# One DMA for each key page and each tile of key rows, in a decoder step on one core

## The chip, the cores and the metric

The kernel runs on one core of a Trainium2 chip. The time is the device time of one execution in microseconds. A core has TensorE (PE in the profile; PEld is its loading of weights), VectorE (DVE), ScalarE (ACT), GpSimd (POOL) and SyncE (SP), each with a list of instructions that it works off in order, and 16 DMA engines that they share. The rows SPq are SP's own queue: it issues DMAs and waits for what they depend on.

## The reference: what is computed

One step of a two-layer decoder trunk in fp32, for a new sequence of 512 tokens and for 8 running sequences of 4 new tokens each with 256 cached tokens. Layer 0 mixes with a convolution module, layer 1 with stick-breaking attention, and each is followed by a gated feed-forward network. What the change touches is in layer 1:

```python
k_past = [jnp.take(cache_k[a], page_table, axis=0).reshape(db, past_len, N_HEADS, HEAD_DIM) ...]
qkv = (h @ attn_w_qkv[a]).reshape(b, t, 3, N_HEADS, HEAD_DIM)
z = jnp.einsum('bqhd,bkhd->bhqk', q, k) * (HEAD_DIM ** -0.5) + bias
log_fail = jnp.where(valid, jax.nn.log_sigmoid(-z), 0.0)
after = lax.cumsum(log_fail, axis=3, reverse=True) - log_fail
weights = jnp.where(valid, jnp.exp(jax.nn.log_sigmoid(z) + after), 0.0)
out = jnp.einsum('bhqk,bkhd->bqhd', weights, v)
```

The cached keys lie in pages of 128 tokens x 16 heads x 64 floats (512 KB); each running sequence has two pages, named by a table, so there are 16. The key rows of the new tokens, 512 x 1024 floats for the long sequence, are an output too (k_p).

## The kernel before

Activations are kept transposed, features on the 128 partitions and 544 tokens (512 + 32) along the free axis, in 8 chunks of 128 features. Weights come in loads of up to 1 MB (`raw`, two buffers, L361), which ACT and DVE split into a high and a low part (L398, L401) for matmuls in three products.

From the attention on (L2111 to L2565) the order of the work is made by a planner, `Plan`. Each step is put down with an engine, a cost in us, and what it reads and writes; `run` (L192) then lists the steps greedily by their estimated times and emits them in that order, so each engine's list is fixed when the program is built. For a step of SP the cost says when its result is there, while SP itself is taken to be free again after 0.7 us (L242). A step with an engine name of its own, such as the flight of a page (L2261, 6.0 us), only delays its users.

Key pages. `key_page` (L2041) fetches a page into one of three buffers in xT, which is free at that time because its content was saved to DRAM (L1896). Pages 0 to 2 are asked for ahead of the attention (L1901), pages 3 to 15 in it (`page`, L2251), each when its buffer has been read. The fetch makes four DMAs, one for each column group x of four heads: partitions 32x to 32x+31 take the tokens 32q + p in four blocks q of 256 floats. DVE transposes the page in blocks of 32 x 32 (L2283), so that the head features lie on partitions, and PE multiplies it with the queries (L2301): `page_logits(m)` does four pages, m = 0 to 3, in matmuls of 128 or 256 columns. After the key pages the value pages come through the same three buffers by POOL's indirect DMAs (L2050).

Key rows. `keys(c, h)` projects the keys of chunk c for half h of the tokens (16 tiles in all). ACT copies the result to kT (L2201), DVE transposes the 256 columns into `kr` (two buffers, L2207), and `store` (L2209) writes it to k_p with four DMAs, one for each 32 features. In DRAM a token's 32 features are a run of 128 B.

Other DMAs that matter for the argument. All go through SP's queue in the order of its list: the weight loads of L361, the stores of values (L2228), and in layer 0 the stores of L1181, which write 32 partitions (8 sequences x 4 tokens) to a DRAM tensor in which the sequences lie 30 rows apart:

```python
dst = sc_s[0, :, PAST - NI:PAST, :].rearrange("b t (h j d) -> b t h j d", h=2, j=4)
nc.sync.dma_start(out=dst[:, :, :, j, :], in_=r)
```

Of the kernel before, what the change touches and what calls it, by code (L numbers as in the profile page):

```python
# [17 lines left out]
P = 128  # L18
D = 1024
NC = D // P  # L20
# [85 lines left out]
class Plan:  # L106
# [5 lines left out]
    def __init__(self, eager=EAGER, chain=0.0, shifts=""):  # L112
        self.eager = eager
        self.shifts = shifts

        self.chain = chain
        self.ops = []
        self.writes, self.adds, self.reads = {}, {}, {}
        self.rings = {}
        self.follows = {}  # L120
        self.lift, self.urgent = {}, {}
        self.forms, self.change = {}, 0.0
        self.fill = set()

    def op(self, eng, cost, fn, r=(), w=(), a=(), follows=None, lift=0.0, urgent=0.0, after=(), form=None):

        i = len(self.ops)
        deps = set(after)
        for x in r:
            deps |= self.writes.get(x, set()) | self.adds.get(x, set())  # L130
        for x in a:
            if self.reads.get(x):
                self.writes[x] = self.writes.get(x, set()) | self.reads[x] | self.adds.get(x, set())
                self.reads[x], self.adds[x] = set(), set()
            deps |= self.writes.get(x, set())
        for x in w:
            deps |= self.writes.get(x, set()) | self.reads.get(x, set()) | self.adds.get(x, set())
        for x in r:
            self.reads.setdefault(x, set()).add(i)
        for x in a:  # L140
            self.adds.setdefault(x, set()).add(i)
        for x in w:
            self.writes[x], self.reads[x], self.adds[x] = {i}, set(), set()
        for x in (*r, *w, *a):
            b = x[0] if isinstance(x, tuple) else x
            if isinstance(b, Plan.Buf):
                if not b.users and b.before is not None:
                    b.after |= {b.before.users[0]}
                if not b.users and b.old is not None:
                    b.after |= set(b.old.users)  # L150
                deps |= b.after
                b.users.append(i)
        deps.discard(i)
        self.ops.append((eng, cost, fn, deps))
        if lift:
            self.lift[i] = lift
        if urgent:
            self.urgent[i] = urgent
        if follows is not None:
            self.follows[i] = follows  # L160
        if form is not None:
            self.forms[i] = form
        return i

    class Buf:
# [26 lines left out]
    def run(self):  # L192
        n = len(self.ops)
        users = [[] for _ in range(n)]
        left = [0] * n
        for i, (_, _, _, deps) in enumerate(self.ops):
            left[i] = len(deps)
            for d in deps:
                users[d].append(i)
        rank = [0.0] * n  # L200
        for i in range(n - 1, -1, -1):
            eng, cost, _, _ = self.ops[i]
            rank[i] = cost + self.lift.get(i, 0.0) + max((rank[u] + self.lag(eng, self.ops[u][0]) for u in users[i]), default=0.0)
        for x in self.shifts.split():
            i, d = x.split(":")
            self.urgent[int(i)] = self.urgent.get(int(i), 0.0) + float(d)
        ready = {}
        start = [0.0] * n
        for i in range(n):
            if not left[i]:  # L210
                ready.setdefault(self.ops[i][0], []).append(i)
        free, last, form = {}, {}, None

        def turned(i):
            return self.change if self.change and self.ops[i][0] == "pe" and self.forms.get(i) != form else 0.0

        while any(ready.values()):
            best = None
            for eng, q in ready.items():
                if q:  # L220
                    f = free.get(eng, 0.0)
                    soon = min(max(f, start[i]) for i in q) + NEAR

                    def key(i):
                        t, turn = max(f, start[i]), turned(i)
                        later = t > soon or i in self.fill or (turn and self.fill and form is None and start[i] + PATIENT > soon)
                        return (bool(later), t + CHANGE_BIAS * turn - self.eager * rank[i] - self.urgent.get(i, 0.0) -
                                (STICK if self.follows.get(i, -1) == last.get(eng) else 0.0), i)

                    i = min(q, key=key)  # L230
                    t = max(f, start[i])
                    if best is None or t < best[0]:
                        best = (t, i, eng)
            t, i, eng = best
            ready[eng].remove(i)
            _, cost, fn, _ = self.ops[i]
            fn()
            cost += turned(i)
            if eng == "pe":
                form = self.forms.get(i)  # L240
            last[eng] = i
            free[eng] = t + (cost if eng != "sp" else 0.7)  # L242
            for u in users[i]:
                left[u] -= 1
                start[u] = max(start[u], t + cost + self.lag(eng, self.ops[u][0]))
                if not left[u]:
                    ready.setdefault(self.ops[u][0], []).append(u)
# [3 lines left out]
def tile_trunk(  # L251
# [8 lines left out]
    nc = tc.nc  # L260
    dve, act, pool, pe = nc.vector, nc.scalar, nc.gpsimd, nc.tensor
# [1778 lines left out]

    def key_page(t, j):  # L2041

        pages = cache_k[0, bass.ds(numbers[j], 1)].rearrange("o (q p) (x h) d -> o x p q (h d)", p=32, x=4)
        for x in range(4):
            nc.sync.dma_start(out=t[32 * x:32 * x + 32, :].rearrange("p (q r) -> p q r", q=4), in_=pages[0, x])

    cv = cache_v.rearrange("o n p h d -> (o n p) (h d)")

# [149 lines left out]
    def keys(c, h):  # L2198
        c0, n = (SA, SB)[h]
        pt = project(k0 + TURNS.index(("k", c)), h)  # L2200
        plan.op("act", acost(256), lambda: act.copy(kT[:, c, c0:c0 + 256], pt()[:, :256]),  # L2201
                r=[pt], w=[("k", c, h)] + ([("ktp", i) for i in range(4)] if c >= 4 else []))
        if h:
            plan.op("act", 0.2, lambda: act.copy(kT_s[:, c, :], pt()[:, 256:n]), r=[pt], w=[("kT_s", c)])
            plan.op("pool", 1.2, lambda: place_k(c), r=[("kT_s", c)], w=[("kn", c)])
        kr = sbuf("kr", 2 * P, 2)
        plan.op("dve", 0.15 + 256 * 1.1e-3, lambda: dve.transpose(kr(), kT[:, c, c0:c0 + 256]), r=[("k", c, h)], w=[kr])  # L2207

        def store():  # L2209
            for a in range(4):  # L2210
                rows = slice(32 * a, 32 * a + 32)
                nc.sync.dma_start(out=k_p[0, 0, c0:c0 + 256].rearrange("(b i) h d -> i b (h d)", i=32)[:, :, c * P + 32 * a:c * P + 32 * a + 32],
                                  in_=kr()[rows].rearrange("i (b j) -> i b j", j=32))

        plan.op("sp", 7.0, store, r=[kr])

    def values(c, h):
        n = (SA, SB)[h][1]
# [12 lines left out]
    def new_rows(src, r, dst):  # L2231

        rows = psum("one")

        def turn():
            for x in range(4):
                for j in range(2):
                    pe.matmul(rows()[HALF[j], x * HD:(x + 1) * HD], src[HALF[j], 2 * x:2 * x + 2, :].rearrange("p c t -> p (c t)"),
                              ident[HALF[j], HALF[j]], start=(x == 0), stop=(x == 3), skip_group_check=True)

        def store():
            for u in range(4):
                nc.sync.dma_start(out=dst.rearrange("t (x u d) -> t u x d", x=4, u=4)[:, 2 * (u % 2) + u // 2],
                                  in_=new_s[32 * u:32 * u + 32].rearrange("p (x d) -> p x d", x=4))

        plan.op("pe", 0.5, turn, r=r, w=[rows], form="r64")
        plan.op("act", 0.35, lambda: act.copy(new_s, rows()[:, :2 * P]), r=[rows], w=["new", "Qz"])
        plan.op("sp", 3.0, store, r=["new"])


    def page(i):  # L2251
# [3 lines left out]
            plan.op("held", 0.0, lambda: None, w=[t])  # L2255
            return t
        if i < 2 * NB:
            plan.op("sp", 2.0, lambda: key_page(t(), i), w=[t, ("asked", i)])
        else:
            plan.op("pool", 1.05, lambda: gather(t(), i % (2 * NB), cv), w=[t, ("asked", i)])  # L2260
        plan.op(f"page{i}", 6.0 if i < 2 * NB else 4.0, lambda: None, r=[("asked", i)], w=[(t, 1)])  # L2261
# [8 lines left out]
    def page_logits(m):  # L2270
# [17 lines left out]
        def logits():  # L2288
            for odd in range(2):
# [5 lines left out]
                    parts = [(0, KW, kt)]  # L2295
                for e in range(2):
                    for lo, n, src in parts:
                        keys_of = src.rearrange("p (q k j) -> p k q j", k=NC, j=32)
                        for u in range(4):
                            k = 4 * (u % 2) + 2 * (u // 2) + e  # L2300
                            pe.matmul(z()[32 * u:32 * u + 32, (m % 2) * KW + lo:(m % 2) * KW + lo + n],  # L2301
# [322 lines left out]
```

## Time and profile before

| | |
|---|---|
| time, median of 3 runs | 1256.89 us (1256.1 to 1257.56) |
| the profiled execution's own time | 1256.83 us |
| its span, first to last instruction | 1255.1 us |
| PE, DVE, ACT, POOL busy | 1239.3, 1011.2, 709.8, 173.8 us |
| granted PE clock | 0.998 |
| DMA packets of SP's queue | 133134 (120.29 MB) |
| key page DMAs / key row DMAs | 64 x 128 KB / 64 x 32 KB |

A row of a group or of the timeline gives line, engine and operation, then out<-in by the program's names. In square brackets stands the idle time just before an instruction, and what ended it. DMA share is the mean busy share of the 16 DMA engines; "share of 16 engines" is the time that a queue's packets took, over 16 times the length of the window.

### The profile page before, as it was taken

To read this page: it belongs to the slowest core of one execution; us is meant where nothing else is said; L and a number is where in the kernel's file an instruction comes from. 1 tells how busy PE (TensorE), PEld (TensorE's weight loads), DVE (VectorE), ACT (ScalarE), POOL (GpSimd) and SP (SyncE) were. 2 spreads that over 40 slices of the span, in tenths; PEclk is the share of its full clock that TensorE was granted. 3 is DMA by queue.
4 is the path that set the end of the run, shared out by engine and by line. 5 is a ranking of instruction groups with operands and counts; after the bars stand their busy time and mean duration, and the time that the engine had idled before them with its cause. 6 is when DMAs were issued, how large, how long until landed. Compare 5 with 4: busy or idle time off the path is not lost.

```text
span 1255.1 us, 26652 instructions
## 1 busy us (share of the span) xinstructions
PE 1239.3 (99%) x10742; PEld 1187.2 (95%) x10742; DVE 1011.2 (81%) x1700; ACT 709.8 (57%) x1421; POOL 173.8 (14%) x363
## 2 busy tenths in 40 slices
PE   9999999999999999999999999999999999999997
PEld 8997699999999999999988888999999999999997
DVE  7999887988987886878969897646979987887863
ACT  7793584646655454445545887744636645455453
POOL 5000014111001000000242344000101001000000
PEclk9999999999999999999999999999999999999999
DMA  7455423123233233244379465232123232233121
GB/s 223 129 168 152 129 68 117 35 86 114 80 112 118 68 106 99 92 145 161 97 190 246 128 173 159 71 126 85 49 88 102 93 120 93 80 108 118 60 79 72
DMA packets 139661, 142.40 MB, mean 113 GB/s; under 512 B 24045, under 2 KB 132773, under 8 KB 139266
## 3 DMA queue, kind: packets, MB, share of 16 engines
q1 hardware_dynamic: 133134, 120.29, 32.1%
q0 software_dynamic: 6400, 20.41, 5.2%
q8 instruction: 84, 1.38, 0.5%
q14 instruction: 39, 0.32, 0.1%
q10 hardware_dynamic: 4, 0.01, 0.0%
HBM read 129.34 MB, written 12.18 MB: 113 GB/s over the span
## 4 chain that ended last, share of the span: by engine, by line
PE 81%; DVE 14%; DMA 2%; ACT 2%; issue 1%; SPq 0%; POOL 0%; DVEq 0%; ACTq 0%
PE acc L1635 5%; PE acc L1634 5%; PE acc L1633 5%; PE acc L759 4%; PE acc L760 4%; PE acc L761 4%; PE av L896 3%; DVE wlo L401 3%; PE av L1412 3%; PE av L1413 3%; PE av L1414 3%; PE tr L1413 3%; PE tr L1412 3%; PE tr L1414 3%; PE tr L1633 3%; PE tr L1635 3%
## 5 line engine op out<-in xcount | busy, mean ns | idle before, releaser
L398 ACT CAST whi<-raw 128x1024 fp32r<-128x1024 f32 (+2 forms) x247 | 224.7, 913 | 123.5 <-PE av L1413 24.8
L401 DVE TENSOR_TENSOR wlo<-raw,whi 128x1024 fp32r<-128x1024 f32 (+2 forms) x247 | 258.7, 1050 | 33.0 <-ACT whi L398 31.5
L759 PE MATMUL acc<-XH,whi 128*128 128x288 f32 (+1 forms) x384 | 112.7, 294 | 0.0
L761 PE MATMUL acc<-XH,wlo 128*128 128x288 f32 (+1 forms) x384 | 110.3, 287 | 0.9 <-DVE wlo L401 0.9
L760 PE MATMUL acc<-XL,whi 128*128 128x288 f32 (+1 forms) x384 | 110.3, 287 | 0.0
L1412 PE MATMUL av<-HH,whi 128*128 128x288 f32 (+1 forms) x280 | 83.2, 297 | 0.5 <-DVE xT L1735 0.5
L1413 PE MATMUL av<-HL,whi 128*128 128x288 f32 (+1 forms) x280 | 82.6, 295 | 0.0
L1635 PE MATMUL acc<-TH,wlo 128*128 128x272 f32 x288 | 82.6, 287 | 0.0
L1634 PE MATMUL acc<-TL,whi 128*128 128x272 f32 x288 | 82.6, 287 | 0.0
L1633 PE MATMUL acc<-TH,whi 128*128 128x272 f32 x288 | 82.5, 287 | 0.0
L1414 PE MATMUL av<-HH,wlo 128*128 128x288 f32 (+1 forms) x280 | 82.2, 293 | 0.0
L1682 ACT COPY G<-acc 128x272 f32<-128x272 f32 (+1 forms) x72 | 26.8, 372 | 93.8 <-PE acc L1635 93.8
L2163 PE MATMUL acc<-XH,whi 128*128 128x256 f32 (+1 forms) x264 | 79.7, 302 | 0.0
L1412 PE MATMUL tr<-HH,whi 128*128 128x256 f32 (+1 forms) x280 | 78.5, 280 | 0.0
L1413 PE MATMUL tr<-HL,whi 128*128 128x256 f32 (+1 forms) x280 | 78.4, 280 | 0.0
L1414 PE MATMUL tr<-HH,wlo 128*128 128x256 f32 (+1 forms) x280 | 78.3, 280 | 0.0
L2165 PE MATMUL acc<-XH,wlo 128*128 128x256 f32 (+1 forms) x264 | 75.7, 287 | 0.0
L2164 PE MATMUL acc<-XL,whi 128*128 128x256 f32 (+1 forms) x264 | 75.7, 287 | 0.0
L759 PEld LDWEIGHTS acc<-XH,whi 128*128 128x128 f32 x384 | 72.2, 188 | 1.4 <-issue 0.4
L761 PEld LDWEIGHTS acc<-XH,wlo 128*128 128x128 f32 x384 | 72.1, 188 | 1.1 <-DVE wlo L401 1.1
L760 PEld LDWEIGHTS acc<-XL,whi 128*128 128x128 f32 x384 | 72.2, 188 | 0.3
L1573 DVE SCALAR_TENSOR_TENSOR cv<-G,fprm,cv 128x560 f32<-128x560 f32 x88 | 69.5, 797 | 0.5
(464 smaller groups left out, 4343.0 us busy)
## 6 DMA issues: line engine op xcount, KB each, us to landing
raw<-in_ffn_w_gate_dram SPq DMA_DIRECT2D x22, 1024.0 KB
raw<-in_ffn_w_up_dram SPq DMA_DIRECT2D x22, 1024.0 KB
raw<-in_ffn_w_down_dram SPq DMA_DIRECT2D x24, 768.0 KB
raw<-in_attn_w_qkv_dram SPq DMA_DIRECT2D x12, 1024.0 KB
xT<-in_cache_k_dram SPq DMA_DIRECT2D x64, 128.0 KB
raw<-in_conv_w_in_dram POOLq DMA_DIRECT2D x6, 1024.0 KB, 6.8
rep<-glu SPq DMA_DIRECT2D x36, 142.0 KB
raw<-in_conv_w_out_dram POOLq DMA_DIRECT2D x4, 1024.0 KB, 6.4
```

Of the source, the lines that this page charges most:

```text
L398: act.copy(hi[:, k, :], src[:, k])
L401: dve.tensor_tensor(lo[:, k, :], src[:, k], hi[:, k, :], op=ALU.subtract)
L759: pe.matmul(o, hi[:, k, :], XH[:, k, c0:c0 + n], start=(k == 0), stop=False)
L760: pe.matmul(o, hi[:, k, :], XL[:, k, c0:c0 + n], start=False, stop=False)
L761: pe.matmul(o, lo[:, k, :], XH[:, k, c0:c0 + n], start=False, stop=(k == NC - 1))
L1412: pe.matmul(o, hi[:, j + k, :], xh, start=(start and k == 0), stop=False, **kw)
L1413: pe.matmul(o, hi[:, j + k, :], xl, start=False, stop=False, **kw)
L1414: pe.matmul(o, lo[:, j + k, :], xh, start=False, stop=(stop and k == len(xs) - 1), **kw)
L1633: pe.matmul(o, hi[:, j + k, :], xh, start=(start and k == 0), stop=False, **kw)
L1634: pe.matmul(o, hi[:, j + k, :], xl, start=False, stop=False, **kw)
L1635: pe.matmul(o, lo[:, j + k, :], xh, start=False, stop=(k == 3), **kw)
L2163: pe.matmul(o, hi[:, k, :], XH[:, k, c0:c0 + n], start=(k == 0), stop=False)
```

## The change

One DMA fetches a page. Token t goes to block t mod 4 of partition 32x + t div 4 instead of block t div 32 of partition 32x + t mod 32, so the page buffer is filled in one sweep of the source. The logits matmuls read their columns in a permuted order (block q innermost), so that the logits come out in token order as before. The same for key rows: the transpose into kr takes every eighth token of the 256 into a block, partition i gets the tokens 8i to 8i+7, and one DMA stores the tile, its DRAM side counting the four feature groups, then 256 tokens, then 32 floats. The planner is given new costs for SP's steps, and a `hold`, how long SP itself is taken up, 0.7 us unless given.

```diff
-    def op(self, eng, cost, fn, r=(), w=(), a=(), follows=None, lift=0.0, urgent=0.0, after=(), form=None):
+    def op(self, eng, cost, fn, r=(), w=(), a=(), follows=None, lift=0.0, urgent=0.0, after=(), form=None, hold=0.7):
...
-            free[eng] = t + (cost if eng != "sp" else 0.7)
+            free[eng] = t + (cost if eng != "sp" else self.hold[i])
...
     def key_page(t, j):
-        pages = cache_k[0, bass.ds(numbers[j], 1)].rearrange("o (q p) (x h) d -> o x p q (h d)", p=32, x=4)
-        for x in range(4):
-            nc.sync.dma_start(out=t[32 * x:32 * x + 32, :].rearrange("p (q r) -> p q r", q=4), in_=pages[0, x])
+        nc.sync.dma_start(out=t, in_=cache_k[0, bass.ds(numbers[j], 1)].rearrange("o t (x h) d -> (o x) t (h d)", x=4))
...
         kr = sbuf("kr", 2 * P, 2)
-        plan.op("dve", 0.15 + 256 * 1.1e-3, lambda: dve.transpose(kr(), kT[:, c, c0:c0 + 256]), r=[("k", c, h)], w=[kr])
+        plan.op("dve", 0.15 + 256 * 1.1e-3, lambda: dve.transpose(kr().rearrange("p (b i) -> p b i", i=32), kT[:, c, c0:c0 + 256].rearrange("p (i b) -> p b i", i=32)), r=[("k", c, h)], w=[kr])
 
         def store():
-            for a in range(4):
-                rows = slice(32 * a, 32 * a + 32)
-                nc.sync.dma_start(out=k_p[0, 0, c0:c0 + 256].rearrange("(b i) h d -> i b (h d)", i=32)[:, :, c * P + 32 * a:c * P + 32 * a + 32],
-                                  in_=kr()[rows].rearrange("i (b j) -> i b j", j=32))
-        plan.op("sp", 7.0, store, r=[kr])
+            nc.sync.dma_start(out=k_p[0, 0, c0:c0 + 256].rearrange("t h d -> t (h d)")[:, c * P:(c + 1) * P].rearrange("t (a j) -> a t j", a=4),
+                              in_=kr())
+        plan.op("sp", 5.0, store, r=[kr])
...
         plan.op("act", 0.35, lambda: act.copy(new_s, rows()[:, :2 * P]), r=[rows], w=["new", "Qz"])
-        plan.op("sp", 3.0, store, r=["new"])
+        plan.op("sp", 4.0, store, r=["new"], hold=1.9)
...
-            plan.op("sp", 2.0, lambda: key_page(t(), i), w=[t, ("asked", i)])
+            plan.op("sp", 0.7, lambda: key_page(t(), i), w=[t, ("asked", i)])
...
-                        keys_of = src.rearrange("p (q k j) -> p k q j", k=NC, j=32)
+                        keys_of = src.rearrange("p (g q k j) -> p k g j q", q=4, k=NC, j=32)
```

More of the change, by code (lines that the diff above doesn't have):

```diff
@@ L123, in __init__ @@
         self.fill = set()
-    def op(self, eng, cost, fn, r=(), w=(), a=(), follows=None, lift=0.0, urgent=0.0, after=(), form=None):
+        self.hold = {}
+    def op(self, eng, cost, fn, r=(), w=(), a=(), follows=None, lift=0.0, urgent=0.0, after=(), form=None, hold=0.7):
         i = len(self.ops)
@@ L162, in op @@
             self.forms[i] = form
+        self.hold[i] = hold
         return i
```

## The prediction, on record before the changed kernel ran

> **What bounds the kernel now.** I read the page's first part, then the table of stretches over the place where the changed lines run, then the instructions of the DMA-issuing queue (SPq) and of DVE in order of time, and last the DMA view of short windows.
>
> ```profile
> span 1255.1 us, 26652 instructions
> PE 1239.3 (99%) x10742; PEld 1187.2 (95%) x10742; DVE 1011.2 (81%) x1700; ACT 709.8 (57%) x1421; POOL 173.8 (14%) x363
> 637.14:692.08 54.94, 52.09 (x521) 46.05 (x520) 44.11 (x53) 27.53 (x50) 19.17 (x63) 1.00 0.96 235
> 700.00:760.00 60.00, 60.00 (x559) 49.32 (x558) 52.92 (x74) 51.64 (x90) 26.18 (x32) 1.00 0.53 158
> ```
>
> The columns of the last two rows are stretch, length, then busy time of PE, PEld, DVE, ACT, POOL, the granted clock, the DMA share and GB/s. PE is busy 99% of the span, so nothing that makes another engine lighter can give much: in the stretch where the key pages are fetched PE is idle 54.94 - 52.09 = 2.85 us. But in that stretch the 16 DMA engines are busy 0.96 of the time, the most of any part I looked at. PE sets the end with the DMA engines close behind it, and the change is to DMAs. So I count the DMA work there.
>
> ```profile
> 635.98 0.37 SPq L361 DMA_DIRECT2D raw<-in_attn_w_qkv_dram  x1
> 637.14 4.73 SPq L2045 DMA_DIRECT2D xT<-in_cache_k_dram  x8
> 642.06 2.22 SPq L2212 DMA_DIRECT2D out_dram<-kr  x4
> 644.55 0.40 SPq L361 DMA_DIRECT2D raw<-in_attn_w_qkv_dram  x1
> 645.40 2.26 SPq L2212 DMA_DIRECT2D out_dram<-kr  x4
> 647.84 4.95 SPq L2045 DMA_DIRECT2D xT<-in_cache_k_dram  x8
> 652.90 3.84 SPq L2212 DMA_DIRECT2D out_dram<-kr  x8
> 656.98 6.05 SPq L2045 DMA_DIRECT2D xT<-in_cache_k_dram  x12
> 663.14 0.41 SPq L2228 DMA_DIRECT2D out_dram<-vtok  x1
> 663.80 2.94 SPq L2045 DMA_DIRECT2D xT<-in_cache_k_dram  x4
> 666.91 1.81 SPq L2212 DMA_DIRECT2D out_dram<-kr  x4
> 668.96 4.55 SPq L2045 DMA_DIRECT2D xT<-in_cache_k_dram  x8
> 673.61 0.40 SPq L361 DMA_DIRECT2D raw<-in_attn_w_qkv_dram  x1
> 674.26 5.44 SPq L2045 DMA_DIRECT2D xT<-in_cache_k_dram  x8
> 680.55 0.77 SPq L361 DMA_DIRECT2D raw<-in_attn_w_qkv_dram  x1
> 682.05 0.41 SPq L2228 DMA_DIRECT2D out_dram<-vtok  x1
> 682.85 2.21 SPq L2045 DMA_DIRECT2D xT<-in_cache_k_dram  x4
> ```
>
> ```profile
> 644.03 1.25 DVE L2283 STREAM_TRANSPOSE e<-xT 128x1024 f32<-128x1024 f32 x1 [2.91 <-DMA xT<-in_cache_k_dram]
> ...
> 692.08 1.25 DVE L2283 STREAM_TRANSPOSE e<-xT 128x1024 f32<-128x1024 f32 x1 [2.08 <-DMA xT<-in_cache_k_dram]
> ```
>
> L2045 counts 52 = 13 pages of four DMAs; pages 0 to 2 came earlier. Between them in the same queue lie five tiles of key rows (L2212, 20 DMAs), four weight loads with the one at 635.98, and two stores of values. A page has three buffers, so page i+3 is asked for only when DVE has transposed page i (L2283). Already now the pages are late twice in the rows shown: DVE, which works in order, waits 2.91 us for page 3 and 2.08 us for page 15, the last, whose transpose starts at 692.08. The logits of the last pages (L2301) follow it on PE.
>
> **On how many engines a DMA runs.** The DMA view of a window counts packets; besides data it has small ones.
>
> ```profile
> DMA packets 1731, 1.61 MB, mean 161 GB/s; under 512 B 192, under 2 KB 1728, under 8 KB 1728
> ...
> q1 hardware_dynamic: 1728, 1.57, 67.6%
> ```
>
> ```profile
> DMA packets 1040, 1.05 MB, mean 175 GB/s; under 512 B 16, under 2 KB 1040, under 8 KB 1040
> ...
> q1 hardware_dynamic: 1040, 1.05, 53.4%
> ```
>
> ```profile
> DMA packets 288, 0.13 MB, mean 43 GB/s; under 512 B 32, under 2 KB 288, under 8 KB 288
> ```
>
> ```profile
> q1 hardware_dynamic: 1432, 0.18, 43.4%
> ```
>
> ```profile
> q1 hardware_dynamic: 144, 2.23, 87.8%
> ```
>
> The windows are 592 to 602 us (the first three pages), 622 to 628 (one weight load), 191.3 to 194.35, 655 to 657.5 (stores of key rows) and 586 to 592 (the 2.2 MB save of xT, 128 packets of 17 KB). Twelve page DMAs leave 192 small packets, 16 each; the weight load leaves 16. The third window holds the four 32 KB stores of L1181 (288 - 32 = 256 data packets, 512 B each): 32 small packets, 8 each. I take the small packet as the mark that each engine sets at the end of its share. L1181 writes a DRAM pattern whose outermost count is 8 (sequences) from 32 partitions; a page DMA has 32 outermost on both sides. So the outermost counts of the two sides decide: 8 against 32 gives 8 engines. No run shows a count of 4.
>
> **The change, part by part.**
>
> *The page DMA.* The new pattern counts on the DRAM side 4 column groups outermost, then 128 tokens, then 256 floats, against 128 partitions in SBUF. By the reading above it runs on 4 engines instead of 16. Its 512 packets of 1 KB are then 128 on each of four. Price of a packet: the weight load, also 1 KB each, took 0.534 x 6 us x 16 / 1024 = 50 ns; today's page packets took 0.676 x 10 us x 16 / 1536 = 70 ns, 16 engines writing the same 32 partitions at once; the save took 0.878 x 6 us x 16 / 128 = 658 ns for 17 KB, 39 ns per KB. New: 50 ns, because each engine has 32 partitions to itself, which is nearer to the weight load; ends 39 and 70. A page is 128 x 50 ns = 6.4 us of the four engines (5.0 to 9.0), where it was 512 x 70 ns / 16 = 2.2 us of all.
>
> *The store of key rows.* Outermost 4 against 128 partitions again, so 1024 packets of 128 B are 256 on each of four. Price 0.434 x 2.5 us x 16 / 1432 = 12.1 ns, so 3.1 us.
>
> *The sum.* SP's DMAs go through an engine in the order of issue, so the four engines have to do, up to the end of page 15: 13 pages x 6.4 = 83.2; five tiles of key rows x 3.1 = 15.5; four weight loads, 64 packets of 50 ns each = 3.2, 12.8; two stores of values, by bytes a quarter of a weight load, 1.6. Together 113.1 us. Two pages are always queued behind the one awaited, so I count no gaps; a store of key rows now queues behind pages and holds its kr buffer, and with it DVE, longer, but the pages asked for go on arriving meanwhile. Counted from the issue of the weight load at 635.98, page 15 is there at 749.1 instead of about 692.1: 57.0 us later. DVE is in order and its other work between the pages (44.11 us in the stretch, transposes included) doesn't depend on how late they are; PE's list stands between those steps, and after the stretch PE has nothing left to catch up with (60.00 of 60.00 us). So the shift goes to the end: 1255.1 + 57.0 = 1312.1 us of span, and 1.7 us around it, as in the profiled run (1256.83 against 1255.1); that run stands 0.06 us below the median of 1256.89. Forecast 1313.8, say 1314. With 39 ns per KB the sum is 64.9 + 15.5 + 10.0 + 1.6 = 92.0, page 15 at 728.0 and the time 1293; with 70 ns for page packets 116.5 + 15.5 + 12.8 + 1.6 = 146.4, 782.4 and 1347.
>
> *What SP saves.*
>
> ```profile
> L2045 SPq DMA_DIRECT2D xT<-in_cache_k_dram x64: 316/317/1395, 592.0 to 684.7; - x64
> L2212 SPq DMA_DIRECT2D out_dram<-kr x64: 315/446/1957, 642.1 to 785.9; - x64
> L2207 DVE STREAM_TRANSPOSE kr<-kT x16: 403/436/447, 639.3 to 783.3; 128x256 f32<-128x256 f32 x16
> ```
>
> 48 page issues and 48 row issues fall away: 48 x 0.317 + 48 x 0.446 = 36.6 us of SP. SP is waited for only through the transfers, so alone this is worth at most the 2.85 us of PE idle.
>
> *Strided reads.* The transpose of key rows now reads every eighth float, and L2301 steps 1 KB from one column to the next. On DVE the bounds are 0 and a doubling, 16 x 0.436 = 7.0 us; 11 of the 16 come after the pages, where DVE has 60 - 52.92 = 7.1 us free. I take 0 for the end. On PE I take 0 too and price the other end as a rival.
>
> *The planner.* It is told 0.7 us for a page issue instead of 2.0, 5.0 instead of 7.0 for a row store, and 4.0 with 1.9 held for L2248. It keeps 6.0 us for a page's flight and knows of no shared engine, so its new order can't foresee the queue. A changed order may move the end a few us either way; that lies inside the range.
>
> **Rivals.** *The transfer is spread as before (ends on the other side: faster).* If 4 against 128 is still dealt to 16 engines, a page takes 512 x 50 ns / 16 = 1.6 us instead of 2.2 and DVE's waits for pages go. The gain is at most the 2.85 us of PE idle: 1254, and 1257 if the waits only move to the next late input. The point from which it decides: the other terms of the sum are 29.9 us, so a page may cost its engines (54.94 - 29.9) / 13 = 1.9 us before the stretch grows; four engines need 5.0 even at 39 ns. The Trainium skill speaks for this rival: "DMA: Bandwidth & Descriptors", Rules for kernel authors, says to join small transfers into one and that transfers to separate partition groups only queue behind each other; by that rule alone the time is this rival's. Against it stand the 8 marks of L1181.
>
> *The strided read on PE doubles the logits.* Four blocks of L2301 take 1.87 us each in the chain that ended last:
>
> ```profile
> 665.04 1.87 PE dz L2301 x48
> ```
>
> Doubled, 4 x 1.87 = 7.5 us, all on PE: with pages as fast as now, 1264. No row here has such a read on PE, so nothing of the trace speaks for it or against it; the chance is small because it counts only where the pages come on time. The Trainium skill, "SBUF — State Buffer", Door 1: The DMA port swizzle, says that each step to another 16-byte line is charged and that two hits on a line are needed for full rate; it gives no number, and taken as a doubling it gives these 1264 us. In the forecast's case three of the four blocks lie in time that PE spends waiting.
>
> **How the numbers follow.** Four engines: 0.82; spread as before: 0.13 (within 0.2% 0.08, faster 0.05); strided PE read with spread pages: 0.05. A measurement of this kernel tells about 0.2%, 2.5 us, from no change. Slower by more: 0.82 + 0.05 = 0.87. The range is that of the first case with a few us for the new order, 1290 (from 1293) to 1348 (from 1347); it leaves out the other 0.18.
>
> **What would show it.** Right: page DMAs of 512 KB with 4 small packets each; a DMA share under a half in the page stretch, since twelve engines have little to do; DVE waits for xT from the cache of some 50 us in total, with L2283's last start near 750; PE idle there by as much, and after it the stages as long as before. Wrong: 16 small packets per page, or pages that land in under 4 us on four engines; a shift that is caught up again by 823 us; or L2301 blocks longer than 1.87 us while pages are on time.

## The result, and the profile after

The changed kernel takes 1318.38 us (median of 6 runs, 1317.96 to 1324.52) against 1257.32 (6 runs, 1256.1 to 1258.16) on the same chip: 1.0493 times as long, 95% interval 1.0474 to 1.0513. It is slower by 61.1 us. The profiled execution took 1318.25 us, with a span of 1316.6.

First the stretch of the page loads, from the first page issue that waits for a buffer to the start of the last page's transposition, and the time after it. Both are rows of the table of stretches; the first fence is the changed kernel, the second the one before. The columns are stretch, length, busy time of PE, PEld, DVE, ACT and POOL, granted clock, DMA share, GB/s.

```profile
637.84:752.31 114.47, 71.53 (x541) 59.65 (x543) 45.62 (x53) 28.93 (x52) 20.40 (x67) 0.81 0.43 116
752.31:860.00 107.69, 107.58 (x1050) 90.25 (x1042) 90.59 (x130) 82.85 (x147) 39.13 (x53) 1.00 0.49 136
```

```profile
637.14:692.08 54.94, 52.09 (x521) 46.05 (x520) 44.11 (x53) 27.53 (x50) 19.17 (x63) 1.00 0.96 235
692.08:800.00 107.92, 107.56 (x1073) 90.94 (x1073) 88.68 (x131) 84.17 (x150) 41.33 (x57) 1.00 0.49 139
```

The stretch grew from 54.94 to 114.47 us: 59.5 of the 61.5 us of span. It also starts 0.7 us later, and 1.3 us come after it. PE is idle for 114.47 - 71.53 = 42.9 us of it (2.85 before); the other 19.4 us are busy time that got longer, at a granted clock of 0.81 as the mean of the stretch. The DMA engines look *less* loaded than before, 0.43 against 0.96. That is the row to read carefully: a share is a mean over sixteen engines, and for work that only four of them may do it stays near 4/16 however long the queue is (27.1% at 706 to 711 us, where pages alone are loaded). The DMA view of the first three pages, alone in their window (592.5 to 613.8 us), shows it:

```profile
DMA packets 1551, 1.61 MB, mean 75 GB/s; under 512 B 12, under 2 KB 1548, under 8 KB 1548
...
q1 hardware_dynamic: 1548, 1.57, 23.0%
```

3 x 512 = 1536 data packets and 12 small ones: 4 marks per page DMA, where the kernel before had 16. The share is 23.0%, that is 0.230 x 16 = 3.7 engines, as a mean over a window with idle edges. A packet of 1 KB took 0.230 x 21.3 us x 16 / 1536 = 51 ns, so a page takes 128 x 51 ns = 6.5 us. The Trainium skill, "DMA: Bandwidth & Descriptors", section "Why a DMA increments its semaphore by 16 and not by 1", says that a DMA runs on the largest number up to 16 that divides the slowest loop of both its sides; by it 4 against 128 gives 4, and the 4 marks here agree.

What waits for this, in the changed kernel's waits of DVE (total us, times, longest), 637 to 753 us, and in its order of time:

```profile
DVE e L2281 <- DMA xT<-in_cache_k_dram: 37.8, 7, 9.7
DVE kr L2207 <- DMA out_dram<-kr: 20.6, 3, 13.3
DVE kT L2281 <- DMA xT<-in_cache_k_dram: 8.0, 2, 4.4
```

```profile
752.31 1.25 DVE L2281 STREAM_TRANSPOSE e<-xT 128x1024 f32<-128x1024 f32 x1 [7.31 <-DMA xT<-in_cache_k_dram]
```

DVE waits 45.8 us for pages and 20.6 us until a store has let go of its kr buffer. The last page is transposed at 752.31 instead of 692.08. PE waits behind both: 23.1 us for DVE (L2465) and 18.0 for ACT (L2219), and ACT in turn waits 30.2 us for DVE's scans (L2460). The chain that ended last runs through the stretch almost on transfers alone (start, length, what):

```profile
637.84 11.29 DMA xT<-in_cache_k_dram
649.13 13.48 DMA out_dram<-kr
662.61 13.40 DMA xT<-in_cache_k_dram
...
677.29 11.23 DMA xT<-in_cache_k_dram
...
689.82 15.85 DMA xT<-in_cache_k_dram
...
717.98 18.53 DMA xT<-in_cache_k_dram
...
738.50 13.72 DMA xT<-in_cache_k_dram
```

SP has fewer DMAs to issue, but not less to do. The rows give an issue's ns, minimum, median and maximum:

```profile
L2045 SPq DMA_DIRECT2D xT<-in_cache_k_dram x16: 587/3226/7189, 592.7 to 738.5; - x16
L2210 SPq DMA_DIRECT2D out_dram<-kr x16: 571/1286/7760, 649.1 to 845.5; - x16
```

A page took four issues of 0.32 us. It now takes one of 3.2 us in the median, with a minimum of 0.59. We read this as SP being held while the queues of the four engines are full; no run tests that by itself. Of the 13 pages in the stretch, SP's blocks of issues add up to 51.3 us (11.25 + 4.96 + 16.82 + 11.84 + 3.64 + 2.81) where they were 30.9 us.

### The profile page after: what moved, and what is told of

It reads as the page before. It is cut to its first block, busy times and chain, and to the rows that moved or that the text cites. A ratio compares the mean times of both kernels' runs of the same rounds, so it can differ in the third digit from the quotient of the medians.

```text
span 1316.6 us, 26417 instructions
## 1 busy us (share of the span) xinstructions
PE 1260.2 (96%) x10742; PEld 1201.3 (91%) x10742; DVE 1015.1 (77%) x1700; ACT 708.8 (54%) x1421; POOL 174.2 (13%) x363
## 3 DMA queue, kind: packets, MB, share of 16 engines
q1 hardware_dynamic: 131214, 120.28, 30.2%
## 4 chain that ended last, share of the span: by engine, by line
PE 76%; DVE 13%; DMA 8%; issue 1%; ACT 1%; DVEq 0%; ACTq 0%; SPq 0%
DMA xT<-in_cache_k_dram 6%; PE acc L1637 5%; PE acc L1636 5%; PE acc L1635 5%; PE acc L761 3%; PE acc L762 3%; PE acc L763 3%; PE av L898 3%; DVE wlo L403 3%; PE av L1414 3%; PE av L1415 3%; PE av L1416 3%; PE tr L1415 2%; PE tr L1414 2%; PE tr L1416 2%; PE tr L1635 2%
## 5 line engine op out<-in xcount | busy, mean ns | idle before, releaser
L2163 PE MATMUL acc<-XH,whi 128*128 128x256 f32 (+1 forms) x264 | 83.3, 315 | 0.1
```

The source lines that it names most:

```text
L2163: pe.matmul(o, hi[:, k, :], XH[:, k, c0:c0 + n], start=(k == 0), stop=False)
```

## Experiments

Theory: the cost comes from the four engines, page DMAs above all. Rivals: the planner's new order (its costs changed too); the strided reads of PE and DVE that the new layout needs; the row stores rather than the pages. Each kernel was timed against the kernel before on the same chip.

**Undoing one part: all in fours, pages alone as one, rows alone as one.** The new layout, transposes, column order and planner costs stay.

```diff
-        nc.sync.dma_start(out=t, in_=cache_k[0, bass.ds(numbers[j], 1)].rearrange("o t (x h) d -> (o x) t (h d)", x=4))
+        pages = cache_k[0, bass.ds(numbers[j], 1)].rearrange("o t (x h) d -> x (o t) (h d)", x=4)
+        for x in range(4):
+            nc.sync.dma_start(out=t[32 * x:32 * x + 32, :], in_=pages[x])
...
-            nc.sync.dma_start(out=k_p[0, 0, c0:c0 + 256].rearrange("t h d -> t (h d)")[:, c * P:(c + 1) * P].rearrange("t (a j) -> a t j", a=4),
-                              in_=kr())
+            for a in range(4):
+                nc.sync.dma_start(out=k_p[0, 0, c0:c0 + 256].rearrange("t h d -> t (h d)")[:, c * P + 32 * a:c * P + 32 * a + 32],
+                                  in_=kr()[32 * a:32 * a + 32])
```

Both edits (all in fours):

> The changed layout, strided reads and planner costs, but four DMAs again for each page and each tile of key rows, each with 32 partitions against 128 or 256 tokens outermost. Engine theory (the time goes where a DMA runs on 4 engines): 16 small packets per DMA, the pages as fast as before, 1257 to 1262 us, the few us above 1257 being what the strided reads cost (L2299 took 658 ns for 256 columns after against 379 before, in part at a lower clock). Rival (the strided reads and the permuted order cost it): stays within 5 us of 1318.

The second edit alone (pages stay one DMA):

> Key rows with four DMAs on 16 engines, pages with one DMA on 4. Engine theory by the sum: up to the last page six tiles of rows were in the queue after the change, and each falls from 3.1 to 0.8 us of the four engines: 13.8 us less, 1304 us (1300 to 1310). Rival (DVE's 20.6 us of waiting for kr is an extra beside the pages): 1297. Rival (strided reads): 1318.

The first alone (rows stay one DMA):

> Pages with four DMAs on 16 engines, key rows with one DMA on 4 engines. Engine theory: the four engines have 13 x 2.2 + 6 x 3.1 + 9.6 + 1.6 = 58 us to do in a stretch of 55, so page 15 is late by a few us: 1258 to 1266. Rival (a single DMA is slow whatever its load): most of the way back to 1318.

Measured: all in fours 1274.22 us (ratio 1.0137, 1.012 to 1.0154); pages as one 1310.7 (1.0421, 1.0403 to 1.0438); rows as one 1274.23 (1.0138, 1.0117 to 1.0159). The pages carry most of the loss: in four DMAs each they give back 44.2 us of the 61.1, whether the rows go as one DMA or as four. A row store on four engines costs nothing while the pages are in fours, and 1318.4 - 1310.7 = 7.7 us behind pages on four engines. Pages as one came out 0.7 us above its range, rows as one 8 us above, and all in fours 12 us above its own (1257 to 1262), 16.2 us above the kernel before. That last miss is taken up below.

**Changing the number of engines.** One DMA per page, its outermost loop not 4 but 16 or 8. The size and number of packets change with it: a packet holds one head (256 B) or two (512 B); these kernels put the page in other places of the tile.

```diff
-        nc.sync.dma_start(out=t, in_=cache_k[0, bass.ds(numbers[j], 1)].rearrange("o t (x h) d -> (o x) t (h d)", x=4))
+        nc.sync.dma_start(out=t, in_=cache_k[0, bass.ds(numbers[j], 1)].rearrange("o t (x h) d -> (o x) t (h d)", x=16))
```

> Still one DMA per page and per tile of rows, but the page's DRAM side counts 16 groups of one head outermost instead of 4 groups of four heads: 2048 packets of 256 B. The page lies wrongly in its buffer, so the sample's output is not the reference's; all the work is done. Engine theory: 16 small packets per page; a 256 B packet at some 25 ns (an estimate between 12 ns for 128 B and 50 ns for 1 KB) makes 128 x 25 = 3.2 us on each of 16 engines, and the sum 13 x 3.2 + 18.6 + 9.6 + 1.6 = 71 us against 115: about 1318 - 44 = 1274 (1262 to 1285). Rival (it is the single DMA, or its four-times longer list of packets, that is slow): 1318 or more.

The same with x=8:

> As the one with 16 groups, with 8 groups of two heads: 1024 packets of 512 B, the page again misplaced in its buffer. Engine theory: 8 small packets per page; a 512 B packet at some 32 ns makes 128 x 32 = 4.1 us on each of 8 engines, sum 13 x 4.1 + 29.8 = 83 us: about 1286 (1275 to 1297), between the kernels with 4 and with 16 groups. Rival: 1318 or more.

Measured: 1275.49 us with 16 (1.0147, 1.0131 to 1.0162), 1292.18 with 8 (1.0282, 1.0266 to 1.0298), both within the ranges given. The DMA view of the first three pages, first with 16 (592.5 to 613.4 us), then with 8 (593 to 613.6):

```profile
DMA packets 6195, 1.61 MB, mean 77 GB/s; under 512 B 6192, under 2 KB 6192, under 8 KB 6192
...
q1 hardware_dynamic: 6192, 1.57, 51.9%
```

```profile
DMA packets 3099, 1.61 MB, mean 78 GB/s; under 512 B 24, under 2 KB 3096, under 8 KB 3096
...
q1 hardware_dynamic: 3096, 1.57, 40.3%
```

6192 - 6144 = 48 marks are 16 per page, and 24 are 8 per page. Packets of 256 B took 0.519 x 20.9 x 16 / 6144 = 28 ns, those of 512 B 0.403 x 20.6 x 16 / 3072 = 43 ns. An engine has 128 packets of a page in each case, so a page takes 3.6 us on 16 engines, 5.5 on 8 and 6.5 on 4. Still one DMA, and with 16 engines it is as good as four: the single DMA is not the cost, its outermost loop is. That bears the theory out, although the 16-group DMA moves four times as many packets. With 8 groups the range was met partly by luck: a packet was expected at 32 ns, and at 43 ns the same sum gives 13 x 5.5 + 29.8 = 101 us instead of 83, or 1304. So the price of the first three pages seems too high for pages that follow one another closely; for four engines the sum below shows the same.

**The planner's costs, alone and undone.** On the kernel before, only the new costs (with the lines for `hold`, shown under the change):

```diff
-        plan.op("sp", 7.0, store, r=[kr])
+        plan.op("sp", 5.0, store, r=[kr])
...
-        plan.op("sp", 3.0, store, r=["new"])
+        plan.op("sp", 4.0, store, r=["new"], hold=1.9)
...
-            plan.op("sp", 2.0, lambda: key_page(t(), i), w=[t, ("asked", i)])
+            plan.op("sp", 0.7, lambda: key_page(t(), i), w=[t, ("asked", i)])
```

> The kernel before with the new planner costs alone. Engine theory: the order hardly matters, 1257 within 3 us. Rival (the new order of the lists brings the loss): several tens of us.

The reverse of this diff on the changed kernel:

> The changed kernel with the planner costs of before. Engine theory: 1318 within 5 us, since the four engines have the same DMAs to carry up to the last page. Rival (the new order brings the loss): back towards 1257.

Measured: 1263.0 us (1.0051, 1.0038 to 1.0065) for the kernel before with the new costs, so 5.9 us slower, above what was expected. In the changed kernel the old costs give 1316.99 (1.0475, 1.0459 to 1.0491), whose interval overlaps the changed kernel's (1.0474 to 1.0513). The new order does cost, but where four engines already set the pace the median moves by only 1.4 us.

**Why all in fours is at 1274.** Two parts of the change that the theory had left at little or nothing are the order (above) and the strided reads. This kernel takes the reads of PE back: all in fours, with the columns read where they lie.

```diff
-                        keys_of = src.rearrange("p (g q k j) -> p k g j q", q=4, k=NC, j=32)
+                        keys_of = src.rearrange("p (g q k j) -> p k g q j", q=4, k=NC, j=32)
```

> As the kernel with everything in fours, but L2299 reads its columns packed, 32 floats in a run, so that the cached tokens' logits come out permuted within a page and the sample's output is not the reference's; the amount of work is the same. Theory (the strided read costs PE by the row): the four blocks fall back to 1.87 us each and the time is 3 to 5 us below the kernel with the strided read, about 1257. Rival (the longer rows of L2299 came from the lower clock): no difference between the two.

Measured: 1272.01 us (1.0111, 1.0094 to 1.0128), 2.2 us below all in fours, less than the 3 to 5 expected and far from 1257; the two intervals just overlap, but no run of one kernel reaches into the runs of the other. The logits matmuls, ns of one, first all in fours, then with packed columns:

```profile
L2302 PE MATMUL dz<-e,xT x128: 396/397/431, 648.5 to 711.6; 128*32 128x128 f32 x128
L2302 PE MATMUL dz<-kT,xT x64: 613/656/786, 646.6 to 709.6; 128*32 128x256 f32 x64
```

```profile
L2302 PE MATMUL dz<-e,xT x128: 272/273/273, 647.0 to 709.5; 128*32 128x128 f32 x128
L2302 PE MATMUL dz<-kT,xT x64: 379/379/404, 646.1 to 708.5; 128*32 128x256 f32 x64
```

The strided read makes one matmul of 128 columns 1.45 and one of 256 columns 1.73 times as long. Matmuls overlap, so the block of a group of four pages says more (start, length, from the chain that ended last; all in fours, then packed):

```profile
674.04 3.91 PE dz L2302 x47
707.87 1.88 PE dz L2302 x48
```

A block takes 2.1 times as long with the strided read, and 1.88 us again without it, as expected. The clock is not the cause, since it is as low in the stretch of page loads with packed columns (0.94) as without (0.95). Over four blocks that is some 8 us more of PE, of which 2.2 reach the end: in all in fours PE is idle 8.2 us of that stretch (68.42 - 60.18, from 638.35 to 706.77 us). Two further kernels take back the planner's order (the reverse of the planner diff, on all in fours) and the way SP issues. All in fours issues a page DMA in 563 ns and a row DMA in 607, where the kernel before took 317 and 446. Rows of the issues, first all in fours, then the kernel before:

```profile
L2047 SPq DMA_DIRECT2D xT<-in_cache_k_dram x64: 562/563/1377, 593.2 to 700.5; - x64
L2213 SPq DMA_DIRECT2D out_dram<-kr x64: 570/607/1847, 647.9 to 805.0; - x64
```

```profile
L2045 SPq DMA_DIRECT2D xT<-in_cache_k_dram x64: 316/317/1395, 592.0 to 684.7; - x64
L2212 SPq DMA_DIRECT2D out_dram<-kr x64: 315/446/1957, 642.1 to 785.9; - x64
```

In fours the new layout reads tokens that follow one another, so one loop of 128 covers the DRAM side while SBUF has 32 partitions. The kernel before has 32 on both. First attempt, the same bytes written with equal loops:

```diff
-        pages = cache_k[0, bass.ds(numbers[j], 1)].rearrange("o t (x h) d -> x (o t) (h d)", x=4)
+        pages = cache_k[0, bass.ds(numbers[j], 1)].rearrange("o (p q) (x h) d -> o x p q (h d)", p=32, x=4)
...
-            nc.sync.dma_start(out=t[32 * x:32 * x + 32, :], in_=pages[x])
+            nc.sync.dma_start(out=t[32 * x:32 * x + 32, :].rearrange("p (q r) -> p q r", q=4), in_=pages[0, x])
```

(and the row stores likewise, "(i b) h d -> i b (h d)" with i=32).

> Four DMAs for each page and row tile in the new layout, as in the run with all in fours, but the two sides of each DMA are written with the same three loops (32 x 4 x 256 for a page, 32 x 8 x 32 for rows): the same bytes to the same places. Theory A, SP's issue of a DMA whose sides are shaped differently is dearer (563 against 317 ns, 64 page DMAs, 52 of them ahead of page 15: 12.8 us): the issue falls back to about 317 ns and the time to about 1265 us (1263.0 with the new planner costs alone, and 2.2 for the strided reads of PE), 1262 to 1268. Theory B, the rest of the loss lies in the strided transposes of DVE or in the addresses of the new layout: no change from 1274.2, within 2 us.

The old order in all in fours:

> All in fours in the new layout, with the planner costs of the kernel before. If the new costs act as they did on the kernel before (1257.1 to 1263.0), the time is about 1268 us (1266 to 1270). If SP's issue is so full that the order no longer matters, as it did not in the changed kernel (1317.0 against 1318.4), it stays at 1274 (1272 to 1276).

Measured: equal loops 1273.49 us (1.0134, 1.0118 to 1.0149), but the issue stayed at 563 and 607 ns. So the run doesn't tell the two theories apart: by the issue times, the way the loops were written changed nothing that SP was given. The old order gives 1268.13 (1.0085, 1.0069 to 1.01), 6.1 us less, the same as the 5.9 that it cost alone.

Second attempt, a source whose loops can't be joined:

```diff
-        pages = cache_k[0, bass.ds(numbers[j], 1)].rearrange("o t (x h) d -> x (o t) (h d)", x=4)
+        pages = cache_k[0, bass.ds(numbers[j], 1)].rearrange("o (p r) (y h) d -> p (o r y) (h d)", p=32, y=2)
         for x in range(4):
-            nc.sync.dma_start(out=t[32 * x:32 * x + 32, :], in_=pages[x])
+            nc.sync.dma_start(out=t[32 * x:32 * x + 32, :].rearrange("p (q r) -> p q r", q=4),
+                              in_=pages[:, 4 * (x // 2):4 * (x // 2) + 4, 256 * (x % 2):256 * (x % 2) + 256])
```

> All in fours in the new layout, but each page DMA reads 32 x 4 pieces of 256 values that lie 512 values apart, so that its loops over 32 and over 4 can't be joined into one over 128 on the DRAM side. The same bytes in the same packets of 1 KB, in other places of the tile: the kernel computes with keys in the wrong places. Theory A, SP's longer issue where the two sides have 128 and 32 as their slowest loops is what the layout costs in fours: a page DMA issues in about 317 ns and not 563, and the time falls from 1274.2 by most of the 9 us that the planner costs and the strided reads of PE leave unexplained, to 1266 (1263 to 1269, since the row DMAs keep their 607 ns). Theory B, the cost lies in the strided transposes of DVE or elsewhere: the issue may fall, the time stays within 2 us of 1274.

Measured: 1269.94 us (1.0095, 1.0078 to 1.0112), 4.3 us below all in fours, a little short of the range of theory A and outside that of B. The issue did fall:

```profile
L2047 SPq DMA_DIRECT2D xT<-in_cache_k_dram x64: 316/317/717, 593.7 to 695.9; - x64
L2214 SPq DMA_DIRECT2D out_dram<-kr x64: 570/607/1788, 646.1 to 801.4; - x64
```

So the cheaper page issue goes with 4.3 us; the run also reads other addresses, and its page packets got dearer (72 ns, see the last section), so this is the worth of the edit rather than of the issue alone. Of the 16.2 us by which all in fours is behind the kernel before (1274.22 - 1258.05), order 6.1, page issue 4.3 and PE's strided reads 2.2 make 12.6, each taken away by itself; that they add up was not tried. 3.6 us stay open. Candidates seen in the trace are the row issue (607 ns against 446) and the transposition into kr; neither was tried alone.

**Something for the kernel before.** Since page packets cost it 70 ns, one attempt to make them cheaper:

```diff
-        for x in range(4):
+        for x in (0, 2, 1, 3):
```

> The kernel before with the four DMAs of a page issued in the order 0, 2, 1, 3. If neighbouring quarters of a tile disturb one another on the way into it, packets of a page get cheaper than the 70 ns of the first pages and the time falls by up to 2.9 us (1254 to 1257). If the order is of no account: 1257 within 1 us.

Measured: 1257.07 us (0.9999, 0.999 to 1.0008). The time did not move, but the packets did get cheaper: over the first three pages (592.9 to 602.9 us) the share is 57.3% where it was 67.6%, 60 ns a packet instead of 70. The order of the four counts for the packets, in one trace of each, and not for the end: DVE still waits 3.7 us for pages in the stretch, 3.1 before. No run here beats the kernel before.

All kernels side by side, with the start of page 15's transposition in the profiled execution and the median time of the runs:

| kernel | page 15 transposed at, us | median time, us |
|---|---|---|
| before, page DMAs in the order 0, 2, 1, 3 | 692.0 | 1257.1 |
| before | 692.1 | 1257.3 |
| before, new planner costs | 698.0 | 1263.0 |
| all in fours, source split | 701.8 | 1269.9 |
| all in fours, old order | 704.5 | 1268.1 |
| all in fours, packed columns | 704.8 | 1272.0 |
| all in fours, equal loops | 705.8 | 1273.5 |
| all in fours | 706.8 | 1274.2 |
| one DMA, 16 groups | 708.3 | 1275.5 |
| pages in fours, rows as one | 708.4 | 1274.2 |
| one DMA, 8 groups | 724.7 | 1292.2 |
| pages as one, rows in fours | 744.8 | 1310.7 |
| changed kernel, old order | 750.9 | 1317.0 |
| changed kernel | 752.3 | 1318.4 |

To within 3 us the last page's lateness is the lateness of the end.

## Why the prediction was right, point by point

*What bounds, and where.* Right. The loss lies in the page stretch and nothing is caught up after it: from page 15 to the end of the span it is 1316.6 - 752.3 = 564.3 us, against 1255.1 - 692.1 = 563.0 before. The share under a half (0.43) and DVE's waits for pages (45.8 us for "some 50") came as forecast too.

*Four engines.* Right: 4 marks per page, 3.7 engines busy, and 16 or 8 marks when the outermost loop is 16 or 8. The price of 50 ns was measured at 51 over the first three pages, and a page at 6.5 us instead of 6.4.

*The sum.* SP's list in the changed kernel up to page 15:

```profile
636.68 0.37 SPq L363 DMA_DIRECT2D raw<-in_attn_w_qkv_dram  x1
637.84 11.25 SPq L2045 DMA_DIRECT2D xT<-in_cache_k_dram  x3
649.13 5.65 SPq L2210 DMA_DIRECT2D out_dram<-kr  x1
654.89 6.69 SPq L363 DMA_DIRECT2D raw<-in_attn_w_qkv_dram  x1
661.62 0.73 SPq L2210 DMA_DIRECT2D out_dram<-kr  x1
662.61 4.96 SPq L2045 DMA_DIRECT2D xT<-in_cache_k_dram  x1
667.68 9.38 SPq L2210 DMA_DIRECT2D out_dram<-kr  x2
677.29 16.82 SPq L2045 DMA_DIRECT2D xT<-in_cache_k_dram  x4
694.24 5.44 SPq L2226 DMA_DIRECT2D out_dram<-vtok  x1
700.26 11.84 SPq L2045 DMA_DIRECT2D xT<-in_cache_k_dram  x3
712.14 5.60 SPq L363 DMA_DIRECT2D raw<-in_attn_w_qkv_dram  x1
717.98 3.64 SPq L2045 DMA_DIRECT2D xT<-in_cache_k_dram  x1
721.66 6.62 SPq L2210 DMA_DIRECT2D out_dram<-kr  x1
728.32 9.19 SPq L2226 DMA_DIRECT2D out_dram<-vtok  x1
737.63 0.62 SPq L2210 DMA_DIRECT2D out_dram<-kr  x1
738.50 2.81 SPq L2045 DMA_DIRECT2D xT<-in_cache_k_dram  x1
```

The queue held 6 row tiles and 3 weight loads up to page 15, not 5 and 4, since the planner had reordered it. With the prediction's prices that is 83.2 + 18.6 + 9.6 + 1.6 = 113.0 us; from the weight load's issue at 636.68 to 752.31 it took 115.6. "No gaps" was right as far as the share can tell: in pieces of 3 us the stretch never shows one under 0.27, about what four busy engines give. Its reason, two pages always queued, was not: DVE stood at the kr buffer, and SP issued a single page between 649.09 and 677.29, while row stores and weight loads kept the four engines busy. That the sum is so near is partly luck. One row tile more and one weight load fewer cancel (3.1 against 3.2 us). A page that follows others closely took less than 6.4 us: at 706 to 711 us the four engines finish 456 packets in 5 us, so 5.6 us a page, and 13 such pages would be some 10 us less. And POOL's first value pages, 3.2% of the engines' time in the stretch or 3.7 us of each, are not in the sum. What else fills the 115.6 us was not followed. Page 15 was put at 749.1 and came at 752.3, the time at 1314 and came at 1318.4.

*The key rows.* Spread over 16 engines, six tiles should have freed 6 x (3.1 - 0.8) = 13.8 us of the four engines; the end came 7.7 us earlier. In part this is because "no gaps" no longer holds there: with the rows in fours the DMA share drops to 0.17 at 673 to 676 us and to 0.21 at 730 to 733. They hold DVE as foreseen, through the kr buffer, for 20.6 us. What else makes up the difference was not followed.

*PE's idle time "by as much".* This failed as put. PE was idle 42.9 us, 40.1 more than before, not 57. The other 19.4 us appear as busy time, with 541 matmuls in place of 521 and a granted clock of 0.81. The two together are the growth of the stretch; we take it that PE has time to be slow while it waits.

*What SP saves.* The 36.6 us of issue were counted as a saving worth little. SP got nothing: held by the full queues, it spent 51.3 us on the stretch's pages. That this changed no time, since SP is waited for only through the transfers, is argued and not tested.

*The strided reads.* Taken at nothing, with a doubling of PE's block as the rival's price. PE's matmul grew 1.73 times, DVE's transposition into kr from 436 to 644 ns. For the changed kernel the end fits the reason given, that PE waits anyway; packed columns were not tried there. The rival's doubling was about right for PE (a block of 3.91 us for 1.88, so some 8 us more for four), and its 7.5 us at the end were not seen: with the pages in fours the reads cost 2.2 us. With pages as early as in the kernel before, which is what the rival supposed, they were not measured. The Trainium skill, "SBUF — State Buffer", Door 1: The DMA port swizzle, charges each step to another 16-byte line without a number; the blocks agree that there is a charge, here about a doubling (2.1 times).

*The planner.* "A few us either way" holds for the kernel before (5.9 us slower) and for all in fours (6.1). In the changed kernel the two medians are 1.4 us apart, with overlapping intervals.

*What the prediction did not see.* With the pages on 16 engines the rest of the change makes the kernel slower all the same: 1275.5 us with 16 groups and 1274.2 in fours, not the 1254 to 1257 of the first rival. One page DMA of 1 KB packets on 16 engines, which is what that rival supposed, was not run. Its argument, that engine time per page is all that counts, missed that the order of SP's list, PE's reads and, in fours, SP's issue come next once the transfer is cheap.

## What to carry to other kernels

Before joining DMAs, read the outermost loop of both sides: here the number of engines came from it (4, 8 and 16 marks for loops of 4, 8 and 16), and one DMA on four engines cost more than four DMAs on sixteen. When a DMA share falls while waits for DMA grow, count the marks and the engines, not the share. Costs off the bounding resource don't add to the loss, but they come back when the bound is lifted: undoing the worst part of this change gave back 44 us of 61.

## What the runs showed of the hardware beyond the prediction

SP's issue of a DMA of 128 packets takes 317 ns with 32 loops on both sides and 563 ns with 128 against 32, and the time is the same whichever way the loops are written if they can be joined. Issues next to it get longer too: a weight load behind such DMAs took 0.53 to 0.55 us instead of 0.40.

The price of a 1 KB page packet went with how fast DMAs follow one another. All in fours writes the same 32 partitions with 16 engines as before, which the prediction gave as the reason for 70 ns. But in the window of the first three pages its share is

```profile
q1 hardware_dynamic: 1744, 1.57, 25.5%
```

over 20.5 us, so 0.255 x 20.5 x 16 / 1536 = 54 ns. Here a page DMA comes every 0.80 us (9.62 us for 12) and keeps an engine for 8 x 54 ns = 0.43. Before, one came every 0.52 us (6.29 us for 12) and took 8 x 70 ns = 0.56, longer than that, so that the DMAs ran into one another. The kernel with the split source bears this out: it has the new layout, but a page DMA comes every 0.55 us (6.54 us for 12), and the share over its first three pages (593.7 to 603.7 us) is 68.7%, again 72 ns a packet. It reads other addresses, so it is no clean test. And the pace is not all: in the order 0, 2, 1, 3 a DMA came every 0.51 us (6.17 us for 12) and a packet took 60 ns.

PE's granted clock was 0.81 as the mean of a stretch in which PE was idle 38% of the time, and 1.00 from its end to 860 us.
